# MLP up-projection: eight products with the weights' high part, then eight with the low part

## The chip, the cores and the metric

The kernel runs on one core of one Trainium2 chip. The metric is device time in microseconds (us). A core has five engines with an instruction stream each: the tensor engine (PE in the profile, with its weight loads listed apart as PEld), the vector engine (DVE), the scalar engine (ACT), GpSimd (POOL) and the sync engine (SP), which here issues the DMAs that bring the weights. Products accumulate in PSUM, which the vector and the scalar engine read.

## The reference

Two layers ("layer 0" and "layer 1" below) of a mixer and an MLP over 256 tokens of width 1024, all in float32. The mixer (three kinds of attention and their gates) is not touched. Of the MLP this is what is computed:

```python
def squared_relu_mlp(h, w_up, w_down):          # h (256, 1024), w_up (1024, 4096), w_down (4096, 1024)
    return jnp.square(jax.nn.relu(h @ w_up)) @ w_down
...
        h = rms_norm(x, mlp_norm[l])
        x = x + squared_relu_mlp(h, w_mlp_up[l], w_mlp_down[l])
```

## The kernel before

Every float32 operand is held as a rounded high part and the remainder, the low part, and a product of two such operands is made of three: high times high, high times low, low times high. `three` (lines 210, 211, 212) issues them one behind the other. A weight tile of 512 KB is fetched by a DMA on SP's queue into one of four `raw` buffers, and split by `fetch`: ACT writes the high part (L190, six `whi` buffers) and DVE the low part (L191, six `wlo` buffers).

The MLP goes over 32 tiles f of 128 of the 4096 hidden columns. `up(f)` multiplies tile f's weights with the normalised activations `xm`, k running over eight blocks of the width. `xm.both(k)` is 512 wide, 256 columns of the activations' high part and 256 of their low part, so that one product with the weights' high part (L873, 512 wide) does two of the three, and a second with the low part (L874, 256 wide) the third. Both go into one PSUM tile `u`, named `pup`, of which there are four. For each k the two stand side by side: high, low, high, low. The last tile, f = 31, is done with `three` (`project_t`), whose products are 256 wide here.

`squared_relu(f)` brings the tile out of PSUM: ACT copies one half (L880), DVE adds the other (L881) and applies relu and the norm's row `xm.row` (L882), ACT squares (L883) and rounds to the high part (L229), DVE takes the low part (L230). The result is `h2[f]`, named `sq`. `down(w, h2, t, half, f)` multiplies it with the down-projection's weights into one of four accumulators (quarters, two token blocks by two column halves): three 512 wide products each, twelve for each f. The loop runs `down` two tiles behind `up`, so that a repetition of the middle of the MLP is twelve products of `down` and sixteen of `up`.

At the head of the MLP three tiles of `up` are issued ahead of the loop; between the products of the second stand the two products of the norm's statistics (`xm.stats`, L275, four rows in the profile) and between those of the third the transposes that turn the norm into a row (`xm.stats_row`, L313). At the end the four last tiles of `down` (f = 28 to 31) are done by quarter, in the order that `ends` writes: the first quarter with f = 28, 29 and 30, the second with f = 28, the first with f = 31, the second with the rest, then the third and the fourth. In layer 0, ACT copies a quarter that is done (`copied`, L938), PE transposes it one quarter later (`turned`, L944) and DVE adds it to the residual.

The order on each engine is set by a planner, which takes the instructions that are ready by its own estimate of time; only from the end of the MLP on (`order_pe`) is PE's order the written one. In layer 1 the planner also has four groups of four transposes (`x_rows`, L902) among the repetitions. Each engine executes its instructions in order.

Of the kernel before, what the change touches and what calls it, by code (L numbers as in the profile page):

```python
# [15 lines left out]
S = 256  # L16
NT = S // P
L = 2
KD = D // P
# [106 lines left out]
def trunk(ctx: ExitStack, tc: tile.TileContext, x, wts, consts, gains, gfin, xtok, out):  # L126


    nc = tc.nc
# [34 lines left out]
    def load_w(*key):  # L164

        ahead = 0 if key[:2] == (0, "b0") else AHEAD
        while order and len(loaded) < ahead + 1:
            first = order.pop(0)
            loaded[first] = fetch(first)
        return loaded.pop(key)  # L170
# [29 lines left out]
    def misc_tile(name="misc"):  # L200
        return ps.tile([P, 512], F32, name=name, tag="misc", bufs=4)
# [142 lines left out]
    def project_t(l, key, n, xn, o):  # L344

        wh, wl = load_w(l, key, n, 0)
        for k in range(KD):
            xh, xl = xn.k(k)
            three(o, wh[:, k, :], wl[:, k, :], xh, xl, k == 0, k == KD - 1)
# [175 lines left out]
    def layer(l, xn, before):  # L525
# [300 lines left out]
        xm = []  # L826
# [31 lines left out]
        xm = xm[0]  # L858
# [4 lines left out]
        def up(f, between=None):  # L863

            u = misc_tile("pup")
            if f >= NF - WHOLE:
                project_t(l, "up", f, xm, u[:, 0:S])
                return u
            wh, wl = load_w(l, "up", f, 0)
            for k in range(KD):  # L870
                if between and k in between:
                    between[k]()
                nc.tensor.matmul(u, wh[:, k, :], xm.both(k), start=k == 0, stop=False)  # L873
                nc.tensor.matmul(u[:, 0:S], wl[:, k, :], xm.k(k)[0], start=False, stop=k == KD - 1)  # L874
            return u

        def squared_relu(f, u):
# [10 lines left out]
        def down(w, h2, t, half, f):  # L888

            sl, cs = slice(P * t, P * t + P), slice(512 * half, 512 * half + 512)  # L890
            three(
                accs[2 * t + half], h2[0][:, sl], h2[1][:, sl], w[0][:, 0, cs], w[1][:, 0, cs], f == 0, f == NF - 1
            )
# [15 lines left out]

        h2 = {}  # L910
        first = [up(f, {1: {4: lambda: xm.stats(accs[3])}, 2: {4: xm.stats_row}}.get(f)) for f in range(LAG + 1)]
        for f in range(NF):
            h2[f] = squared_relu(f, first[f] if f <= LAG else up(f))
            if LAG <= f < NF - ENDS + LAG:
                w = load_w(l, "down", f - LAG, 0)
                for q in quarters:
                    down(w, h2[f - LAG], *q, f - LAG)
            if last and f in (8, 12, 16, 20):
                x_rows(*quarters[(f - 8) // 4])
# [4 lines left out]
        def finish(q, fs):  # L924
            for i in fs:
                down(ws[i], h2[NF - ENDS + i], *quarters[q], NF - ENDS + i)


        ends = [lambda: (finish(0, range(3)), finish(1, range(1)), finish(0, range(3, 4)))]
        ends += [lambda: finish(1, range(1, 4)), lambda: finish(2, range(4)), lambda: finish(3, range(4))]  # L930

        if not last:
            xn = Normed(G_ATT + KD * (l + 1))
# [85 lines left out]
    for l in range(L):  # L1019
        xn, before = layer(l, xn, before)  # L1020
# [85 lines left out]
```

## Time and profile before

| | us |
|---|---|
| three timed runs | 861.53, 861.37, 861.49; median 861.49 |
| the profiled execution | 861.24 |
| its span, first to last instruction | 859.5 |
| layer 0's MLP, first `up` product to the first product of its end | 248.79 to 417.07 |
| layer 1's MLP, likewise | 672.13 to 841.96 |

The profile is of one execution. A row of the timeline gives an instruction's start and its duration, both in us, the engine, the line, the operation, what it writes and reads, and its shape. Products on PE are pipelined: each is listed as longer than the distance to the next, so the distance from start to start (called the pitch below) is what a product costs, and the durations overlap. A bracket at the end of a row is the time in which the engine was idle before it, and what ended that.

### The profile page before, as it was taken

How to read it: one execution, taken by the hardware profiler on the slowest of the kernel's cores; microseconds unless marked ns; L12 is line 12 of the kernel's file. 1: busy time of each engine (PE TensorE's matmuls, PEld its weight loads, DVE VectorE, ACT ScalarE, POOL GpSimd, SP SyncE). 2: the span in 40 equal slices, each digit the busy share in tenths (PEclk: the TensorE clock that was granted, in tenths of full speed). 3: DMA queues.
4: the chain of work that ended last, by engine and by line, in shares of the span. 5: the costliest groups of instructions: out<-in, count | busy, mean ns of one | idle time of the engine just before them, and what ended most of it. 6: DMA issues, size and time to landing. Idle time of an engine off the chain costs nothing.

```text
span 859.5 us, 12496 instructions
## 1 busy us (share of the span) xinstructions
PE 849.2 (99%) x4544; PEld 728.8 (85%) x4544; DVE 618.1 (72%) x1198; ACT 507.7 (59%) x885; POOL 12.1 (1%) x23
## 2 busy tenths in 40 slices
PE   8999999999999999999999999999999999999997
PEld 7888888988898888888888888889889988888885
DVE  6896787787777666666589767977877776666664
ACT  7766776535456555555577567665355565555553
POOL 0000000000000000000000000000100000000000
PEclk9999999999999999999999999999999999999999
DMA  9775344446366665555356455445565666666641
GB/s 339 235 233 172 124 147 140 148 155 194 126 196 195 202 192 192 183 188 192 109 202 213 153 159 163 139 140 168 150 194 148 174 205 191 190 182 185 196 123 50
DMA packets 42541, 150.08 MB, mean 175 GB/s; under 512 B 4848, under 2 KB 5360, under 8 KB 42480
## 3 DMA queue, kind: packets, MB, share of 16 engines
q1 hardware_dynamic: 42192, 149.13, 55.7%
q8 instruction: 36, 0.59, 0.3%
q10 hardware_dynamic: 288, 0.16, 0.1%
q14 instruction: 25, 0.20, 0.1%
HBM read 148.22 MB, written 1.05 MB: 174 GB/s over the span
## 4 chain that ended last, share of the span: by engine, by line
PE 96%; DVE 1%; ACT 1%; issue 1%; DMA 1%; SPq 0%; POOLq 0%; POOL 0%; ACTq 0%
PE acc L210 22%; PE acc L211 22%; PE acc L212 22%; PE pup L873 13%; PE pup L874 7%; PE po L428 2%; PE ps_s L666 1%; PE ps_pt L421 1%; PE ps_s L388 1%; PE po L429 1%; DMA raw<-wts 1%; ACT whi L190 0%; PE pqk L686 0%; DVE wlo L191 0%; PE ps_r L388 0%
## 5 line engine op out<-in xcount | busy, mean ns | idle before, releaser
L191 DVE TENSOR_TENSOR wlo<-raw,whi 128x1024 fp32r<-128x1024 f32 (+2 forms) x279 | 336.3, 1209 | 164.2 <-ACT whi L190 162.3
L190 ACT ACTIVATE whi<-raw 128x1024 fp32r<-128x1024 f32 (+2 forms) x279 | 292.0, 1048 | 257.7 <-PE acc L212 152.0
L873 PE MATMUL pup<-xs,whi 128*128 128x512 f32 x496 | 176.9, 398 | 0.0
L211 PE MATMUL acc<-wlo,xs 128*128 128x512 f32 (+1 forms) x384 | 151.8, 395 | 0.6 <-DVE wlo L191 0.6
L210 PE MATMUL acc<-whi,xs 128*128 128x512 f32 (+1 forms) x384 | 150.7, 397 | 0.4 <-ACT whi L190 0.3
L212 PE MATMUL acc<-whi,xs 128*128 128x512 f32 (+1 forms) x384 | 150.7, 393 | 0.0
L874 PE MATMUL pup<-xs,wlo 128*128 128x256 f32 x496 | 138.3, 280 | 0.0
L873 PEld LDWEIGHTS pup<-xs,whi 128*128 128x128 f32 x496 | 92.9, 188 | 21.3
L210 PE MATMUL acc<-whi,sq 128*128 128x512 f32 x256 | 101.5, 397 | 0.4 <-ACT sq L229 0.4
L211 PE MATMUL acc<-wlo,sq 128*128 128x512 f32 x256 | 100.0, 391 | 0.0
L212 PE MATMUL acc<-whi,sq 128*128 128x512 f32 x256 | 99.5, 393 | 0.0
L874 PEld LDWEIGHTS pup<-xs,wlo 128*128 128x128 f32 x496 | 93.6, 189 | 2.2
L210 PEld LDWEIGHTS acc<-whi,xs 128*128 128x128 f32 x384 | 72.2, 188 | 14.3 <-ACT whi L190 1.5
L211 PEld LDWEIGHTS acc<-wlo,xs 128*128 128x128 f32 x384 | 72.3, 188 | 14.1 <-DVE wlo L191 1.6
L212 PEld LDWEIGHTS acc<-whi,xs 128*128 128x128 f32 x384 | 72.3, 188 | 13.0
L212 PEld LDWEIGHTS acc<-whi,sq 128*128 128x128 f32 x256 | 47.9, 188 | 11.7 <-DVE sq L230 0.2
L210 PEld LDWEIGHTS acc<-whi,sq 128*128 128x128 f32 x256 | 48.0, 188 | 11.2 <-ACT sq L229 0.8
L211 PEld LDWEIGHTS acc<-wlo,sq 128*128 128x128 f32 x256 | 48.2, 188 | 8.8
L211 PE MATMUL acc<-mTl,whi 128*128 128x256 f32 x128 | 36.3, 284 | 1.0 <-DVE mTl L230 1.0
L210 PE MATMUL acc<-mTh,whi 128*128 128x256 f32 x128 | 36.2, 285 | 0.0
L212 PE MATMUL acc<-mTh,wlo 128*128 128x256 f32 x128 | 36.1, 283 | 0.0
L410 ACT ACTIVATE prob<-prob,smx 128x128 f32<-128x128 f32 x64 | 28.3, 445 | 7.5 <-DVE smx L407 7.2
(241 smaller groups left out, 1196.3 us busy)
## 6 DMA issues: line engine op xcount, KB each, us to landing
raw<-wts SPq DMA_DIRECT2D x268, 512.0 KB, 3.7
raw<-wts SPq DMA_DIRECT2D x7, 416.0 KB, 3.3
xrow<-xtok SPq DMA_DIRECT2D x4, 256.0 KB, 8.4
y<-y SPq DMA_DIRECT2D x4, 256.0 KB, 2.2
DEC<-consts SPq DMA_DIRECT2D x1, 768.0 KB, 7.5
x<-x SPq DMA_DIRECT2D x1, 512.0 KB, 6.3
raw<-wts SPq DMA_DIRECT2D x2, 256.0 KB, 3.7
gf<-gfin SPq DMA_DIRECT2D x1, 512.0 KB, 3.9
```

The source lines that it names most:

```text
L190: nc.scalar.activation(hi[:, :sz], raw[:, :sz], AF.Copy)
L191: nc.vector.tensor_sub(lo[:, :sz], raw[:, :sz], hi[:, :sz].bitcast(F32))
L210: nc.tensor.matmul(o, ah, bh, start=start, stop=False)
L211: nc.tensor.matmul(o, ah, bl, start=False, stop=False)
L212: nc.tensor.matmul(o, al, bh, start=False, stop=stop)
L388: nc.tensor.matmul(o, b if swap else a, a if swap else b, start=i == 0, stop=i == 1)
L410: nc.scalar.activation(p[:, a:b], p[:, a:b], AF.Exp, bias=m[:, 2 + i : 3 + i], scale=scale, accum_out=m[:, 4 + i : 5 + i])
L421: nc.tensor.transpose(pt[:, P * i : P * i + P], got["p"][:, src : src + P], ident)
L428: nc.tensor.matmul(dst, v[0], pT[:, 0:S], start=True, stop=False)
L429: nc.tensor.matmul(dst[:, P:S], v[1], pT[:, S : 3 * P], start=False, stop=True)
L873: nc.tensor.matmul(u, wh[:, k, :], xm.both(k), start=k == 0, stop=False)
L874: nc.tensor.matmul(u[:, 0:S], wl[:, k, :], xm.k(k)[0], start=False, stop=k == KD - 1)
```

## The change

For every tile but f = 0 and f = 31, `up` issues the eight products with the weights' high part first and then the eight with the low part. For f = 0 the order stays side by side, and f = 31 isn't concerned. The statistics and the row's transposes stand before the fifth high product, as before, so now with no low product ahead of them. No product is added or removed, and shapes, operands and buffers stay the same. In `ends`, the second quarter's f = 29 moves ahead of the first quarter's f = 31; the two layers share that list.

```diff
-            for k in range(KD):
-                if between and k in between:
-                    between[k]()
-                nc.tensor.matmul(u, wh[:, k, :], xm.both(k), start=k == 0, stop=False)
-                nc.tensor.matmul(u[:, 0:S], wl[:, k, :], xm.k(k)[0], start=False, stop=k == KD - 1)
+
+            jobs = [(part, k) for part in range(2) for k in range(KD)]
+            for part, k in sorted(jobs, key=lambda job: job[1]) if f == 0 else jobs:
+                if part == 0:
+                    if between and k in between:
+                        between[k]()
+                    nc.tensor.matmul(u, wh[:, k, :], xm.both(k), start=k == 0, stop=False)
+                else:
+                    nc.tensor.matmul(u[:, 0:S], wl[:, k, :], xm.k(k)[0], start=False, stop=k == KD - 1)
             return u
...
-        ends = [lambda: (finish(0, range(3)), finish(1, range(1)), finish(0, range(3, 4)))]
-        ends += [lambda: finish(1, range(1, 4)), lambda: finish(2, range(4)), lambda: finish(3, range(4))]
+        ends = [lambda: (finish(0, range(3)), finish(1, range(2)), finish(0, range(3, 4)))]
+        ends += [lambda: finish(1, range(2, 4)), lambda: finish(2, range(4)), lambda: finish(3, range(4))]
```

What the planner makes of it stands in the built programs. On PE, with H for a high and l for a low product of `up`, 0, 1 and 2 for the three 512 wide products of `down`, s for the statistics and r for the row's transposes, the head of the MLP and its first repetitions are (both layers alike, but for layer 1's `x_rows`):

```
before  HlHlHlHlHlHlHlHlHlHlHlHlHlHHlHllHlHlHlHlHHlssHllHlHlHlHlHlHlHlHlHlrr
        HlHlHlHlHlHlHlHlHlHlHlHlHlHlHlHlH01010101lHlHlHlHlHl2222012012... (40 of down in all) HlHl
        012012012012HlHlHlHlHlHlHlHl012012012012HlHlHlHlHlHlHlHl ...
after   HlHlHlHlHlHlHHHHHHHHHHHHHHHHlHHHHHHHlHllssllllllHllllllllHllllllllrr
        HHHHHHHHllllllllHHHHHHHHllllllllHHHHHHHH01010101llll2222012012... (40 of down in all) llll
        012012012012HHHHHHHHllllllll012012012012HHHHHHHHllllllll ...
```

On ACT, in a repetition, the squaring (L883) now stands ahead of the next weight tile's split (L190) where it stood behind it; at the end of layer 0 tile 30's squaring and rounding likewise stand ahead of the second 832 wide split. On DVE a few instructions change places at the head and one at the end of layer 0. The order on SP and POOL, and everything outside the two MLPs, is the same.

## The prediction

> **What bounds the kernel now.** I read the page first: the busy shares, then the chain that ended last by engine and line, then the costliest groups.
>
> ```profile
> PE 849.2 (99%) x4544; PEld 728.8 (85%) x4544; DVE 618.1 (72%) x1198; ACT 507.7 (59%) x885; POOL 12.1 (1%) x23
> ...
> PE 96%; DVE 1%; ACT 1%; issue 1%; DMA 1%; SPq 0%; POOLq 0%; POOL 0%; ACTq 0%
> ...
> L873 PE MATMUL pup<-xs,whi 128*128 128x512 f32 x496 | 176.9, 398 | 0.0
> ...
> L874 PE MATMUL pup<-xs,wlo 128*128 128x256 f32 x496 | 138.3, 280 | 0.0
> L873 PEld LDWEIGHTS pup<-xs,whi 128*128 128x128 f32 x496 | 92.9, 188 | 21.3
> ```
>
> The tensor engine (PE) is the bound: 96% of the chain, and no idle time ahead of either line of the change. So two things can move the end: the distance from one product's start to the next (the pitch), and the few places where PE waits. The listed 398 and 280 ns overlap and are not the price. I took the pitch from PE's timeline, in one repetition of layer 0's MLP, and then in two places that show what the new order will be made of.
>
> ```profile
> 282.73 0.39 PE L873 MATMUL pup<-xs,whi 128*128 128x512 f32 x1
> ...
> 333.07 0.39 PE L873 MATMUL pup<-xs,whi 128*128 128x512 f32 x1
> ...
> 335.88 0.40 PE L210 MATMUL acc<-whi,sq 128*128 128x512 f32 x1
> ...
> 338.66 0.39 PE L873 MATMUL pup<-xs,whi 128*128 128x512 f32 x1
> ...
> 411.38 0.39 PE L873 MATMUL pup<-xs,whi 128*128 128x512 f32 x1
> ```
>
> From 282.73 to 411.38 lie 23 repetitions: 128.65 / 23 = 5.593 us each, without variation (333.07 to 338.66 is 5.59). Of that the eight pairs take 335.88 - 333.07 = 2.81, and the twelve products of the down-projection 338.66 - 335.88 = 2.78.
>
> ```profile
> 272.00 0.39 PE L211 MATMUL acc<-wlo,sq 128*128 128x512 f32 x1
> ...
> 279.03 0.39 PE L212 MATMUL acc<-whi,sq 128*128 128x512 f32 x1
> ```
>
> The same down-projection products, 32 in a row with no 256 wide ones near: 31 distances in 7.03 us, a pitch of 0.2268. Twelve should take 2.72, not 2.78: behind the alternating pairs, the 512 wide products run slow for a while.
>
> ```profile
> 467.29 0.28 PE L210 MATMUL acc<-cTh,whi 128*128 128x256 f32 x1
> ...
> 468.24 0.28 PE L212 MATMUL acc<-cTh,wlo 128*128 128x256 f32 x1
> ...
> 470.04 0.28 PE L212 MATMUL acc<-cTh,wlo 128*128 128x256 f32 x1
> 470.16 0.40 PE L210 MATMUL acc<-whi,xs 128*128 128x512 f32 x1
> ...
> 472.68 0.39 PE L212 MATMUL acc<-whi,xs 128*128 128x512 f32 x1
> ```
>
> This is a mixer stage whose order is like the new one: an even train of 512 wide products, then 24 of 256, then 512 again. The first eight short ones take 468.24 - 467.29 = 0.95 us, and the pitch stays at 0.12 (470.04 to 470.16). The next eleven distances take 472.68 - 470.16 = 2.52, where 11 x 0.2268 = 2.495: a step from short to long costs about 0.025 once and fades.
>
> **The change part by part.**
>
> A repetition. Nothing is added or removed: eight 512 wide and eight 256 wide products and as many weight loads stay. New sum: eight high at 0.2268 = 1.81, eight low 0.95, twelve down 2.52 + 0.227 = 2.75; together 5.51 against 5.593, so 0.08 less. With the front's scheme, 24 such repetitions stand in each layer's steady part. In four of layer 1's, transposes break the train already:
>
> ```profile
> 717.25 0.60 PE L902 MATMUL pxr<-K,x 128*128 128x128 f32 x4
> ```
>
> There I count half: 46 x 0.08 = 3.7 us. Bounds: if the fading after each step is as long as behind pairs (2.78 instead of 2.75 for the twelve), 0.05 and 2.3 us; if the eight low products in a row cost what they cost within pairs (2.81 - 8 x 0.2268 = 1.00), 0.03 and 1.4 us; if both, nothing. Upper end: 5.50, both at the even pitch (20 x 0.2268 + 8 x 0.12), 4.4 us. I take 3.7, since 467 to 473 us has just this pattern.
>
> What hides the rest of a repetition: the copy from PSUM (L880) waits for a tile's last low product in both programs, so it comes no earlier; the squaring moves ahead of a weight split on the scalar engine (ACT), which splits into six buffers and mostly waits for PE to free one. A repetition needs two splits, a rounding, a squaring and a copy:
>
> ```profile
> L190 ACT ACTIVATE whi<-raw 128x1024 fp32r<-128x1024 f32 (+2 forms) x279 | 292.0, 1048 | 257.7 <-PE acc L212 152.0 <-PE pup L873 55.9 <-PE acc L211 21.5
> ...
> L229 ACT ACTIVATE sq<-relu 128x256 fp32r<-128x256 f32 x64 | 25.9, 415 | 1.6
> L883 ACT ACTIVATE relu<-relu 128x256 f32<-128x256 f32 x64 | 25.2, 403 | 5.8 <-DVE relu L882 5.8
> L880 ACT COPY relu<-pup 128x256 f32<-128x256 f32 x62 | 21.5, 354 | 1.0 <-PE pup L874 1.0
> ```
>
> 2 x 1.05 + 0.42 + 0.40 + 0.35 = 3.3 of 5.5 us on ACT, whose idle time ahead of the splits is put down to PE, and a tile's result is needed only two tiles later. If that cover were gone, each us lost on ACT beyond 2.2 would show on PE, 48 times. On SP's queue the same loads stand in the same order; 1 MB per repetition in 1.5% less time is no new load beside the 339 GB/s that the page's first slice shows:
>
> ```profile
> GB/s 339 235 233 172 124 147 140 148 155 194 126 196 195 202 192 192 183 188 192 109 202 213 153 159 163 139 140 168 150 194 148 174 205 191 190 182 185 196 123 50
> ```
>
> The head of the MLP.
>
> ```profile
> 248.79 0.40 PE L873 MATMUL pup<-xs,whi 128*128 128x512 f32 x1
> ...
> 256.40 0.50 PE L275 MATMUL acc<-ones,sqsum 128*128 128x1 f32 x4
> ...
> 260.44 0.38 PE L313 MATMUL acc<-K,ms 128*128 128x128 f32 x2
> ```
>
> Before the statistics stand 22 high and 21 low products: 22 x 0.2268 + 21 x 0.12 = 7.51, and they took 7.61. In the new order 30 high and 10 low stand there, 8.0 us, so the statistics come some 0.5 later; but only 2 high and 22 low follow before the row's transposes, 3.1 instead of 3.67, and those come at 260.4 as now. Tile 0 is complete after 29 high and 8 low: 7.54 + 0.1, at 256.4 as now. The vector engine (DVE) frees its PSUM buffer at
>
> ```profile
> 249.96 1.23 DVE L191 TENSOR_TENSOR wlo<-raw,whi 128x1024 fp32r<-128x1024 f32 x1 [0.21 <-ACT whi L190]
> ...
> 258.72 0.42 DVE L881 TENSOR_TENSOR relu<-pup,relu 128x256 f32<-128x256 f32 x1
> ```
>
> 259.14, and the fifth tile needs it behind the transposes, after 260.5: no wait. The weights of tiles 1 to 3, whose high products now run ahead, are split before the first step is over (the last of six at 251.2). With fewer steps between widths I take 0.1 per layer, 0.2 in all; bounds 0 and 0.3.
>
> The end of layer 0's MLP, the one long stop of PE in it.
>
> ```profile
> 414.07 0.28 PE L874 MATMUL pup<-xs,wlo 128*128 128x256 f32 x1
> ...
> 414.27 0.90 ACT L190 ACTIVATE whi<-raw 128x832 fp32r<-128x832 f32 x1 [0.88 <-PE pup L873]
> ...
> 415.07 0.35 ACT L880 COPY relu<-pup 128x256 f32<-128x256 f32 x1
> ...
> 415.20 1.03 DVE L191 TENSOR_TENSOR wlo<-raw,whi 128x832 fp32r<-128x832 f32 x1 [0.97 <-ACT whi L190]
> ...
> 417.15 0.90 ACT L190 ACTIVATE whi<-raw 128x832 fp32r<-128x832 f32 x1 [1.73 <-PE pup L211]
> ...
> 417.96 0.70 ACT L883 ACTIVATE relu<-relu 128x256 f32<-128x256 f32 x2
> ...
> 418.22 0.39 PE L212 MATMUL acc<-whi,sq 128*128 128x512 f32 x1
> 418.57 0.71 ACT L229 ACTIVATE sq<-relu 128x256 fp32r<-128x256 f32 x2
> 419.02 0.50 PE L210 MATMUL acc<-whi,sq 128*128 128x512 f32 x1 [0.41 <-ACT sq L229]
> ...
> 419.36 0.39 PE L211 MATMUL acc<-wlo,sq 128*128 128x512 f32 x1
> ```
>
> PE's seventh product of the end needs tile 30's rounding. That stood on ACT behind a split which waited until 417.15 for a buffer that tile 31 freed. The stop is (0.80 - 0.227) + (0.34 - 0.227) = 0.69 us. In the new order tile 30's high products end 0.95 earlier, the first 832 wide split with them (it waited for L873), the copy follows tile 30's end (414.2) directly, and squaring and rounding stand ahead of the second split: copy 0.35, DVE's split 1.03 beside it, two DVE steps and two ACT steps of 0.4 each, 3 us with the handovers, so ready near 417.2 against 418.45 wanted. I count the whole 0.7, bounds 0 and 0.7. Late next would be tile 31: it is wanted two triples after tile 30's now, three with the change, which is what the new `ends` gives (0.68 more); I cost that line at nothing, since its own cover, tile 31's rounding, is there in both orders. Moved past it: the first quarter's copy to its transposes,
>
> ```profile
> 421.41 0.59 ACT L938 COPY ydn<-acc 128x512 f32<-128x512 f32 x1 [2.13 <-PE acc L212]
> ...
> 423.25 0.60 PE L944 MATMUL pyd<-K,ydn 128*128 128x128 f32 x4
> ```
>
> now 1.84 from the copy's start to the transposes with 0.59 needed; with a triple less, 1.16: still hidden. Layer 1's end has no transposes and no such stop.
>
> Sum: 3.7 + 0.2 + 0.7 = 4.6 us from the profiled execution's 861.24, so 856.6; the median of the runs is 861.49, 0.25 above, and gives 856.9.
>
> The trace's pitch of 0.2268 depends on what ran before. The Trainium skill ("TensorE: Matmul & The Clock Gate", section "Back-to-back issue gap") has a warm gap of N / 2.4 + 2.5 ns by the width N alone, 215.8 ns for 512 and 109.2 for 256; the trace has 226.8 and 120, and up to 2% more after a step. By that rule the order of the products could change nothing and the sum would be the 0.7 of the stop; this is the second rival below.
>
> **The rivals.**
>
> Long fading: the 512 wide products run slow behind eight short ones as long as behind pairs. For it: 2.78 in every repetition now. Against it: 470.16 to 472.68. It gives 2.3 + 0.2 + 0.7 = 3.2 less, 858.3.
>
> The order is worth nothing on PE: the 0.09 per repetition stick to the place (the neighbours' reads and writes), not to the pairs. For it: the even train at 272 us runs while no pair is there, but also while ACT and DVE have other work. Then only the stop goes: 860.8, not measurable.
>
> Slower: the head stalls. All four PSUM buffers are open while 30 high products run ahead, and the fifth tile's first product waits for tile 0's release. Now that has 260.58 - 259.14 = 1.4 us to spare. Every us beyond costs two, in two layers; it decides once the release is later by 1.4 + (4.6 + 1.7) / 2 = 4.6 us. Against it: tile 0 ends at the same time as now and ACT's order there is unchanged up to the row. At 6 us late: 861.5 - 4.6 + 9.2 = 866.
>
> Eight weight loads in a row behind short products, each listed at 188 ns, would make 0.19 of the pitch; 467.29 to 470.16, where 24 loads stand so, excludes it.
>
> **How the numbers follow.** Forecast 0.71; long fading 0.14; nothing on PE 0.07; slower 0.04; better than forecast (upper bounds together, 856.1) 0.04. About 0.2% (1.7 us) is what a measurement of this kernel tells from no change, and the first two and the last of the cases are beyond it: faster 0.89, same 0.07, slower 0.04. The likeliest gives 856.9. The range takes the upper bounds with the runs' spread at the low end, 855.8, and the long fading with a smaller share of the stop at the high end, 858.9.
>
> **What would show it.** Right: a repetition of 5.51 us in the steady part, twelve down products in 2.75, no idle time near the end's seventh product, and the row's transposes at 260.4. Wrong: a repetition still at 5.59 (then pairs weren't the cause), a pitch over 0.12 within the low products, or idle time of PE before L876 at the head.

## The result, and the profile after

The changed kernel takes 857.61 us (median of five runs, 857.33 to 857.84) against 861.53 (861.37 to 862.01) for the kernel before on the same chip: 0.9952 of the time, 95% interval 0.9940 to 0.9964. The prediction was 856.9, with a range from 855.8 to 858.9. The profiled execution took 857.82, its span 856.0 (861.24 and 859.5 before).

From the page of the changed kernel: the busy shares, the chain, and the two lines of the change in the costliest groups.

```profile
PE 845.4 (99%) x4544; PEld 729.7 (85%) x4544; DVE 618.4 (72%) x1198; ACT 508.6 (59%) x885; POOL 13.9 (2%) x23
...
PE 96%; DMA 1%; DVE 1%; issue 1%; ACT 1%; POOLq 0%; POOL 0%; ACTq 0%
...
L876 PE MATMUL pup<-xs,whi 128*128 128x512 f32 x496 | 125.1, 391 | 0.0
...
L878 PE MATMUL pup<-xs,wlo 128*128 128x256 f32 x496 | 72.2, 282 | 0.0
```

PE is still 96% of the chain, with as many products as before. Its busy time fell by 3.8 us. The groups' 125.1 and 72.2 us (176.9 and 138.3 before) must not be read as a gain of 118 us: durations overlap, and in a train of like products less of each is put down to its group. The distance from start to start is what counts. PE's timeline of the changed kernel, one repetition, and the first and last of 23:

```profile
283.55 0.39 PE L876 MATMUL pup<-xs,whi 128*128 128x512 f32 x1
...
333.17 1.98 PE L876 MATMUL pup<-xs,whi 128*128 128x512 f32 x8
334.98 1.11 PE L878 MATMUL pup<-xs,wlo 128*128 128x256 f32 x8
335.93 0.40 PE L210 MATMUL acc<-whi,sq 128*128 128x512 f32 x1
...
338.68 1.98 PE L876 MATMUL pup<-xs,whi 128*128 128x512 f32 x8
...
410.35 0.39 PE L876 MATMUL pup<-xs,whi 128*128 128x512 f32 x1
```

(410.35 - 283.55) / 23 = 5.513 us a repetition, against 5.593. Its parts are 1.81 (eight high), 0.95 (eight low) and 2.75 (twelve of the down-projection).

The end of layer 0's MLP, ACT and PE:

```profile
412.37 0.90 ACT L190 ACTIVATE whi<-raw 128x832 fp32r<-128x832 f32 x1 [0.45 <-PE pup L876]
...
413.32 0.37 ACT L884 COPY relu<-pup 128x256 f32<-128x256 f32 x1
...
415.23 0.42 ACT L887 ACTIVATE relu<-relu 128x256 f32<-128x256 f32 x1 [1.53 <-DVE relu L886]
...
415.68 0.42 ACT L229 ACTIVATE sq<-relu 128x256 fp32r<-128x256 f32 x1
...
416.00 0.40 PE L210 MATMUL acc<-whi,sq 128*128 128x512 f32 x1
...
416.08 0.90 ACT L190 ACTIVATE whi<-raw 128x832 fp32r<-128x832 f32 x1
...
417.39 0.39 PE L210 MATMUL acc<-whi,sq 128*128 128x512 f32 x1
...
420.31 0.59 ACT L942 COPY ydn<-acc 128x512 f32<-128x512 f32 x1 [2.57 <-PE acc L212]
...
421.47 0.60 PE L948 MATMUL pyd<-K,ydn 128*128 128x128 f32 x4
```

Tile 30's squaring (415.23) and rounding (415.68) now stand ahead of the second 832 wide split (416.08). PE's seventh product (417.39) has no bracket: the stop of 0.69 us is gone. From the quarter's copy to its transposes lie 1.16 us.

Where the time went, in distances that I took from the starts of the same products in both traces (us):

| | before | after | difference |
|---|---|---|---|
| layer 0: first high product to first steady down product (head) | 31.16 | 31.11 | -0.05 |
| layer 0: the 24 steady repetitions | 134.24 | 132.32 | -1.92 |
| layer 0: the 24 down products of its end that hold the stop | 6.184 | 5.471 | -0.71 |
| layer 0's first high product to layer 1's | 423.333 | 420.640 | -2.69 |
| layer 1: its repetitions | 135.80 | 134.21 | -1.59 |
| layer 1's first high product to the last product of all | 180.514 | 178.880 | -1.63 |

The two long distances together are 4.33 us shorter, but the spans differ by only 3.43 (859.46 and 856.03). The rest lies ahead of both MLPs: layer 0's first high product starts at 248.79 before and at 249.69 after, and PE's 100th product already comes 0.92 us later, counted from its first (25.90 us against 24.98). PE's waits in the first 16 us (total, count, longest), of the kernel before and then of the changed one:

```profile
PE acc L211 <- DVE wlo L191: 0.6, 1, 0.6
PE acc L210 <- ACT whi L190: 0.3, 1, 0.3
```

```profile
PE acc L211 <- DVE wlo L191: 1.1, 2, 0.6
PE acc L210 <- ACT whi L190: 0.7, 1, 0.7
```

PE waits there for the splits of the very first weights, 0.9 us longer in the second trace. The change touches no instruction that runs by then, so this is scatter. In eleven more profiles, below, the 100th product comes 25.14 to 27.40 us after the first, with 25.45 and 25.64 in two more of the changed kernel itself; the profile of before had the earliest of all. The median of the timed runs fell by 3.92, between the two figures.

### The profile page after: what moved, and what is told of

Read it like the earlier page. It is cut to its first block, busy times and chain, and to the rows that moved or that the text cites. A ratio compares the mean times of both kernels' runs of the same rounds, so it can differ in the third digit from the quotient of the medians.

```text
span 856.0 us, 12494 instructions
## 1 busy us (share of the span) xinstructions
PE 845.4 (99%) x4544; PEld 729.7 (85%) x4544; DVE 618.4 (72%) x1198; ACT 508.6 (59%) x885; POOL 13.9 (2%) x23
## 4 chain that ended last, share of the span: by engine, by line
PE 96%; DMA 1%; DVE 1%; issue 1%; ACT 1%; POOLq 0%; POOL 0%; ACTq 0%
PE acc L211 22%; PE acc L210 22%; PE acc L212 22%; PE pup L876 13%; PE pup L878 7%; PE po L428 2%; PE ps_s L666 1%; PE ps_pt L421 1%; DMA raw<-wts 1%; PE ps_s L388 1%; PE po L429 1%; PE pqk L686 0%; DVE wlo L191 0%; PE ps_r L388 0%; ACT whi L190 0%
## 5 line engine op out<-in xcount | busy, mean ns | idle before, releaser
L190 ACT ACTIVATE whi<-raw 128x1024 fp32r<-128x1024 f32 (+2 forms) x279 | 292.0, 1049 | 171.6 <-PE acc L212 80.8
L876 PE MATMUL pup<-xs,whi 128*128 128x512 f32 x496 | 125.1, 391 | 0.0
L887 ACT ACTIVATE relu<-relu 128x256 f32<-128x256 f32 x64 | 26.2, 415 | 88.3 <-DVE relu L886 88.3
L878 PEld LDWEIGHTS pup<-xs,wlo 128*128 128x128 f32 x496 | 68.9, 190 | 4.8
L878 PE MATMUL pup<-xs,wlo 128*128 128x256 f32 x496 | 72.2, 282 | 0.0
```

Of the source, the lines that this page charges most:

```text
L190: nc.scalar.activation(hi[:, :sz], raw[:, :sz], AF.Copy)
L887: nc.scalar.activation(s, s, AF.Square)
```

## The experiments

My theory was the prediction's: alternating short and long products slow the 512 wide ones; each step from short to long costs a little that fades (0.025 us behind a short train); and the stop goes because tile 30's rounding gets ahead of a split on ACT. Rivals: the gain sticks to something else in the new order; the new `ends` made it or a part of it; the stop goes by `ends` and not by tile 30. To get rid of the scatter at the start, each run is read by the distances of the table (layer 0's first high product to layer 1's, and from there to the last product) beside its time.

**The two edits apart.** `old_ends` is the changed kernel with the old list, `only_ends` the kernel before with the new one; `after_again` is the changed kernel unaltered, on the chip of `old_ends`.

```diff
 old_ends (against the changed kernel)
-        ends = [lambda: (finish(0, range(3)), finish(1, range(2)), finish(0, range(3, 4)))]
-        ends += [lambda: finish(1, range(2, 4)), lambda: finish(2, range(4)), lambda: finish(3, range(4))]
+        ends = [lambda: (finish(0, range(3)), finish(1, range(1)), finish(0, range(3, 4)))]
+        ends += [lambda: finish(1, range(1, 4)), lambda: finish(2, range(4)), lambda: finish(3, range(4))]
 only_ends (against the kernel before): the same two lines, the other way round
```

> The changed kernel once more, for the first 15 us. In its first profile PE's order and every distance up to the first MLP are as before, but between 8 and 13 us three waits for the first weights were longer and everything behind is 0.9 us late. Theory 'scatter of the first loads': in another execution the lateness is another one (anything from 0 to 1 us), and the span moves by just that, between 855.1 and 856.1. Rival 'the changed kernel starts later': again 0.9 us late at 15 us. In both, a repetition is 5.513 us and the end of layer 0's MLP has no stop; the time lies between 856.8 and 857.8.

> The changed order of the products, with the old order of the four last tiles of the down-projection. Theory 'the second edit is worth nothing': tile 31's rounding is done before either order wants it, no stop of PE at the end of layer 0's MLP, time as the changed kernel within 0.1 us. Rival 'the second edit took the stop away': a wait of 0.3 to 0.7 us for tile 31's or tile 30's result comes back, time 0.3 to 0.7 above the changed kernel.

> The new order of the end with the old order of the products. Theory 'the second edit is worth nothing by itself': repetitions of 5.593, the stop of 0.7 us at the seventh product stays, since the third triple is the same in both orders; time of the kernel before within 0.1 us. Rival: the stop gets shorter by a triple (0.68) and the time is 860.8.

`after_again` took 857.57 us, 0.9947 (0.9935 to 0.9960); `old_ends` 857.49, 0.9948 (0.9934 to 0.9961). Layer 0's distance is 420.646 with the old list and 420.640 with the new, both without the stop. `only_ends` took 861.63, 0.9998 (0.9989 to 1.0007), with 423.333 in layer 0 as in the kernel before, and the stop is there at PE's seventh product:

```profile
417.50 0.90 ACT L190 ACTIVATE whi<-raw 128x832 fp32r<-128x832 f32 x1 [1.73 <-PE pup L211]
...
418.92 0.71 ACT L229 ACTIVATE sq<-relu 128x256 fp32r<-128x256 f32 x2
...
419.37 0.50 PE L210 MATMUL acc<-whi,sq 128*128 128x512 f32 x1 [0.41 <-ACT sq L229]
```

So the second edit is worth nothing in either order. All the gain is in the order of `up`.

**Tile 30 apart.** `not30` leaves tile 30 side by side and does the rest as changed; `only30` has the new order in tile 30 alone.

```diff
 not30
-            for part, k in sorted(jobs, key=lambda job: job[1]) if f == 0 else jobs:
+            for part, k in sorted(jobs, key=lambda job: job[1]) if f in (0, NF - 2) else jobs:
 only30
-            for part, k in sorted(jobs, key=lambda job: job[1]) if f == 0 else jobs:
+            for part, k in sorted(jobs, key=lambda job: job[1]) if f != NF - 2 else jobs:
```

> The changed kernel, but tile 30 has its products side by side as before. The planner then puts tile 30's squaring on ACT behind the second 832 wide split again. Theory 'the stop went because tile 30's squaring stands ahead of that split': the wait of PE at the seventh product of the end of layer 0's MLP is back, about 0.6 to 0.7 us. Rival 'it went because the earlier tiles release their buffers sooner': no wait. Repetitions of 5.513 us in both.

> Side by side as before for all tiles but tile 30, which has eight high and then eight low products; the end in the new order. Theory: repetitions of 5.593 us, no stop at the end of layer 0's MLP, so 0.7 us below the kernel before (860.8). Rival: the stop stays and the time is that of the kernel before.

`not30` has the repetition of 5.513, and the stop again. Its ACT and PE at the end of layer 0:

```profile
417.64 0.90 ACT L190 ACTIVATE whi<-raw 128x832 fp32r<-128x832 f32 x1 [1.73 <-PE pup L211]
...
419.06 0.71 ACT L229 ACTIVATE sq<-relu 128x256 fp32r<-128x256 f32 x2
...
419.51 0.50 PE L210 MATMUL acc<-whi,sq 128*128 128x512 f32 x1 [0.41 <-ACT sq L229]
```

Layer 0's distance is 421.413, 0.77 more than with the change: 0.71 of the stop, and 0.05 in tile 30's own sixteen products. Its single run took 860.23, which says little, since in its profile the 100th product came 27.40 us after the first, the latest of all; the waits of its first 18 us have

```profile
PE acc L210 <- ACT whi L190: 1.9, 2, 1.2
```

`only30` keeps 5.593 in the other tiles and loses the stop:

```profile
417.32 0.42 ACT L229 ACTIVATE sq<-relu 128x256 fp32r<-128x256 f32 x1
...
417.72 0.90 ACT L190 ACTIVATE whi<-raw 128x832 fp32r<-128x832 f32 x1
...
419.03 0.39 PE L210 MATMUL acc<-whi,sq 128*128 128x512 f32 x1
```

Layer 0 takes 422.579, 0.754 less than before. The time is 861.15, 0.9995 (0.9986 to 1.0004): 0.5 us below the kernel before on that chip, too little for the timed runs to tell. The stop thus hangs on tile 30's own order, and not on the earlier tiles. That order is worth 0.75 of the 4.33 us in layer 0: the stop's 0.71, and 0.05 of tile 30's own sixteen products.

**How the products must be grouped.** If a step from short to long costs a fixed amount, fours (two steps a tile) should stand between eights (one) and pairs (eight), and twos (four steps) nearer to the pairs.

```diff
 group4 (group2: // 2)
-            for part, k in sorted(jobs, key=lambda job: job[1]) if f == 0 else jobs:
+            for part, k in sorted(jobs, key=lambda job: (job[1] if f == 0 else job[1] // 4, job[0])):
```

> Four high, four low, four high, four low: two steps from short to long products per repetition instead of one (and eight before). Theory 'each step costs': the second step costs what is left of the fading after four products, 0.02 to 0.03, so a repetition of 5.53 to 5.54 us. Rival 'only strict alternation is slow': 5.51 as with eight. Rival 'the number of steps doesn't count, the fading behind the last one does': 5.51 or 5.55, with the twelve down products at 2.75 or 2.78.

> Two high, two low, four times: four steps per repetition. Theory 'each step costs': 5.55 to 5.57 us, between 5.51 (one step) and 5.593 (eight). Rival 'only strict alternation is slow': 5.51. If a step cost the same however short the runs are, (5.593 - 5.513) / 7 = 0.0115 each, so 5.55 here and 5.525 with groups of four.

PE's timeline of `group4`, a repetition, and then the same of `group2`:

```profile
333.09 1.07 PE L876 MATMUL pup<-xs,whi 128*128 128x512 f32 x4
334.00 0.64 PE L878 MATMUL pup<-xs,wlo 128*128 128x256 f32 x4
334.47 1.09 PE L876 MATMUL pup<-xs,whi 128*128 128x512 f32 x4
335.40 0.63 PE L878 MATMUL pup<-xs,wlo 128*128 128x256 f32 x4
335.87 0.40 PE L210 MATMUL acc<-whi,sq 128*128 128x512 f32 x1
...
338.64 1.07 PE L876 MATMUL pup<-xs,whi 128*128 128x512 f32 x4
```

```profile
333.29 0.61 PE L876 MATMUL pup<-xs,whi 128*128 128x512 f32 x2
333.74 0.40 PE L878 MATMUL pup<-xs,wlo 128*128 128x256 f32 x2
333.98 0.63 PE L876 MATMUL pup<-xs,whi 128*128 128x512 f32 x2
...
336.07 0.40 PE L210 MATMUL acc<-whi,sq 128*128 128x512 f32 x1
...
338.80 0.62 PE L876 MATMUL pup<-xs,whi 128*128 128x512 f32 x2
```

Over 23 repetitions, fours take 5.547 us and twos 5.507, a little less than eights; 5.53 to 5.54 and 5.55 to 5.57 had been expected. With fours, four high products behind four low ones take 335.40 - 334.47 = 0.93, against 334.00 - 333.09 = 0.91 behind other 512 wide products, and twelve down products 2.77: the step costs some 0.02 each time. With twos, two high behind two low take 0.47 against 0.45, so the step costs too; but the eight low products take 0.92 together by their starts, against 0.95, and the twelve down products only 2.73. Their single runs took 859.67 (fours) and 858.40 (twos). Both have the stop at the end of layer 0 again: the 24 down products that hold it take 6.19 us in both, 0.72 and 0.71 more than with the change, with tile 30's rounding behind the second split on ACT. With fours the squaring is ahead of that split and the rounding behind it, and PE waits at the ninth product, for the low part that DVE takes from the rounded one:

```profile
416.04 0.42 ACT L887 ACTIVATE relu<-relu 128x256 f32<-128x256 f32 x1 [1.63 <-DVE relu L886]
...
416.48 0.90 ACT L190 ACTIVATE whi<-raw 128x832 fp32r<-128x832 f32 x1
...
417.29 0.40 ACT L229 ACTIVATE sq<-relu 128x256 fp32r<-128x256 f32 x1
...
418.83 0.50 PE L212 MATMUL acc<-whi,sq 128*128 128x512 f32 x1 [0.37 <-DVE sq L230]
```

A fixed price for each step is refuted: one, two, four and eight steps a tile cost 5.513, 5.547, 5.507 and 5.593.

**Fewer steps, and twos without the stop.** `two_tiles` issues, from f = 3 on, two tiles together: sixteen high, sixteen low, then 24 down products, half a step a tile. `group2_30` has twos, but eights in tile 30.

```diff
 two_tiles
+        def up_two(f):
+            us = [misc_tile("pup") for _ in range(2)]
+            ws = [load_w(l, "up", f + i, 0) for i in range(2)]
+            for i in range(2):
+                for k in range(KD):
+                    nc.tensor.matmul(us[i], ws[i][0][:, k, :], xm.both(k), start=k == 0, stop=False)
+            for i in range(2):
+                for k in range(KD):
+                    nc.tensor.matmul(us[i][:, 0:S], ws[i][1][:, k, :], xm.k(k)[0], start=False, stop=k == KD - 1)
+            return us
...
+            if f > LAG and f % 2 and f < NF - 1:
+                two[f], two[f + 1] = up_two(f)
-            h2[f] = squared_relu(f, first[f] if f <= LAG else up(f))
+            h2[f] = squared_relu(f, first[f] if f <= LAG else two[f] if f in two else up(f))
 group2_30
-            for part, k in sorted(jobs, key=lambda job: job[1]) if f == 0 else jobs:
+            for part, k in sorted(jobs, key=lambda job: (job[1] if f == 0 else job[1] // (8 if f == NF - 2 else 2), job[0])):
```

> From tile 3 on two tiles of the up-projection together: sixteen high, sixteen low, then 24 products of down. One step for two repetitions. Theory 'each step costs 0.02 net': two repetitions take 32 x 0.2268 + ... = 11.006 instead of 11.026, 0.02 less, 12 times a layer, 0.5 us in all: 857.1. Rival 'the planner or the scalar engine makes a wait of it': two results come at once and ACT and DVE are late; PE then idles before a down product and the time is 857.6 or more.

> Two high, two low in turn for all tiles but 30, which has eight and eight. From the traces so far a repetition in twos takes 5.507 us (5.513 with eights), but tile 30 in twos brought the stop of 0.7 back, since the planner put its squaring behind the second 832 wide split. Theory 'each of the two edits acts where it was seen': repetitions of 5.507, no stop, and behind the first loads a program 0.2 to 0.3 us shorter than the changed kernel. Rival 'the stop hangs on the earlier tiles too': it stays, 0.4 above the changed kernel.

> Two tiles together once more, beside the changed kernel on the same chip: two repetitions 11.007 us, 0.4 to 0.5 below the changed kernel in the median, if the scatter of the first loads lets it show.

> The changed kernel beside the two others: repetitions of 5.513 us, no stop; only the first 15 us differ from its other profiles, by 0 to 1 us.

The sixteen and sixteen of `two_tiles` on PE:

```profile
338.21 3.79 PE L921 MATMUL pup<-xs,whi 128*128 128x512 f32 x16
341.84 2.08 PE L924 MATMUL pup<-xs,wlo 128*128 128x256 f32 x16
343.75 0.40 PE L210 MATMUL acc<-whi,sq 128*128 128x512 f32 x1
```

Two repetitions take 11.007 us, where twice the change's 5.513 is 11.026: one step fewer saves 0.02, as the fading behind a train of short products lets expect. The two distances are 420.432 and 178.688, together 0.40 below the changed kernel's. `group2_30` has 5.507, no stop, and 420.546 and 178.688, 0.29 below. Times: `two_tiles` 856.98, 0.9943 (0.9930 to 0.9955); then, on one other chip, `two_tiles_b` (the same kernel) 857.11, 0.9945 (0.9931 to 0.9958), `group2_30` 857.25, 0.9946, and `after_third` (the changed kernel) 857.67, 0.9955 (0.9942 to 0.9967). The traces put both versions ahead of the changed kernel, and the medians are in the same order. The intervals overlap: 0.4 us is less than the scatter of the first loads.

## Why the prediction was right, point by point

*A repetition: 5.51 predicted, 5.513 measured*, with all three parts (1.81, 0.95, 2.75) as read from the mixer stage at 467 us. Of the bounds, neither long fading (2.78 for twelve) nor dearer low products (1.00 for eight) came. That the order makes the difference is shown by the kernels that change nothing else: 5.593, 5.547, 5.513 and 5.507 with the same 28 products of the same widths. The rival by which the order is worth nothing on PE falls with them. The rule that stood beside it is given in its source for an isolated product (the Trainium skill, "TensorE: Matmul & The Clock Gate", "Back-to-back issue gap"); the prediction took it for a rule of a stream. In this stream, with a weight load for each product, the trace disagrees with it: 226.8 ns where it gives 215.8, and 5.593 and 5.513 us for products of equal widths.

The starts of single products show where the time lay. In the pairs before, the eight high products took 1.88 us and the eight low ones 0.93, so the bound with 1.00 for the low products had put the extra on the wrong ones: alternation slows the 512 wide products, to as much as 241 ns instead of 227 (6%, more than the 2% that the prediction names, which is a mean over twelve). Behind the eight low products (at 335.93 us) the next 512 wide ones take 234, 235, 229, 232 and 231 ns and then 227, and behind the 24 short ones in the mixer stage (at 470.16 us, the kernel before) they take the same. Beside them ACT is busy for 0.58 us of these 1.4 us in the first place and for 1.23 in the second, and the DMA share is 0.49 and 0.81. So the slowing goes with what PE ran before, and not with the neighbours' work.

*46 such repetitions, 3.7 us: 3.51 measured.* The step that was mis-sized is "There I count half", for the four repetitions behind layer 1's transposes. Layer 1's repetitions gained 1.59, which is 20 x 0.08: the four gained nothing. Here is one of them in the kernel before, and then one in the changed kernel, with the transposes right ahead of the first row in both:

```profile
717.61 0.48 PE L873 MATMUL pup<-xs,whi 128*128 128x512 f32 x1
...
720.51 0.40 PE L210 MATMUL acc<-whi,sq 128*128 128x512 f32 x1
...
723.25 0.39 PE L873 MATMUL pup<-xs,whi 128*128 128x512 f32 x1
```

```profile
715.57 2.10 PE L876 MATMUL pup<-xs,whi 128*128 128x512 f32 x8
...
718.46 0.40 PE L210 MATMUL acc<-whi,sq 128*128 128x512 f32 x1
...
721.21 1.98 PE L876 MATMUL pup<-xs,whi 128*128 128x512 f32 x8
```

The sixteen products of `up` take 2.90 before and 2.89 after, the twelve behind them 2.75 in both (2.747 before by the unrounded starts). The four such repetitions take 5.65, 5.60, 5.65 and 5.60 before, 5.63, 5.62, 5.63 and 5.62 after. Before, the twelve already ran as fast behind these pairs as behind a train; and after, the eight high products don't run evenly behind the transposes (0.31 us to the second start, then 0.22 to 0.24 each). The rows of before were in its trace and I didn't read on to them.

*The head: 0.2 predicted for both layers, 0.10 measured*, within its bounds. The order of events was as worked out, in the changed kernel's timeline:

```profile
249.69 0.40 PE L876 MATMUL pup<-xs,whi 128*128 128x512 f32 x1
...
257.78 0.50 PE L275 MATMUL acc<-ones,sqsum 128*128 128x1 f32 x4
...
261.31 0.38 PE L313 MATMUL acc<-K,ms 128*128 128x128 f32 x2
```

The statistics come 8.09 after the first high product (7.61 before; 0.5 later was forecast), the row's transposes 11.62 (11.65 before). The stall at the head, the slower rival, did not come.

*The stop: 0.7 predicted, 0.71 measured.* Its mechanism is borne out by every run: in the five kernels that put tile 30's rounding ahead of the second split (the change, `old_ends`, `only30`, `group2_30`, `two_tiles`) there is no stop, in the five that don't (before, `only_ends`, `not30`, `group4`, `group2`) there is one. The gain was nearly lost, though: "ready near 417.2" rests on ACT's order in the changed program, and with fours the planner lets the second split go ahead of tile 30's rounding. In all five kernels without the stop two things go together: tile 30's high products end earlier, and the planner puts the rounding first. In four of them the first split, which those products release, starts 0.83 earlier than before, counted from the end's first product (0.95 was forecast). In `two_tiles` it starts 0.20 later, but all of tile 30 is done twelve down products earlier. With fours the first split starts 0.34 earlier, and the stop is undiminished. So an earlier first split isn't needed, and 0.34 of it isn't enough. Whether the planner's order alone would do was not tried.

*The `ends` line: nothing predicted, nothing measured* in either direction (0.006 us in layer 0). The first quarter's copy is 1.16 us ahead of its transposes, as worked out, and remains hidden.

*The sum: 4.6 predicted, 4.33 measured* in the distances of the two MLPs: 0.2 too much in the repetitions, 0.1 in the head. *What is left:* 857.61 is 0.7 above the 856.9, and the sum explains 0.3 of it. The rest is scatter from run to run and chip to chip, which these runs don't take apart. The prediction's median of the kernel before, 861.49, was of three runs; the medians of more runs are 861.53, 861.95, 861.68 and 861.75. Where both kernels were timed on one chip, their medians differ by 3.92, 4.38 and 4.08, where the distances of the traces give 4.33.

## What to carry to other kernels

Read the cost of an order from a place of the trace that already has that order, by the distance between starts and not by the listed durations; here one stage of another part of the kernel gave the new repetition to within 0.003 us. Where the gain is multiplied by a count, look at each kind of repetition in the count: four that stood behind transposes had nothing to give. Before a profiled execution is taken as the base of a sum, look at its start: here the scatter of the first loads (0.92 us between the two main profiles) was larger than all errors of the sum.

## What was not expected of the hardware

The cost of mixing widths isn't a price for each step. A tile of `up` with twelve down products takes 5.593 us with eight steps from short to long, 5.547 with two, 5.513 with one, and 5.507 with four. Behind pairs of one high and one low the twelve down products take 2.78, behind fours 2.77, behind eights 2.75 and behind twos 2.73; behind transposes and pairs they take 2.75. By the starts of single products, the first ten of the twelve don't run evenly behind pairs (225 to 241 ns), the first nine behind fours (225 to 236), five behind eights (229 to 235), and two behind twos (233 and 231). The short products differ too: the first behind a 512 wide one takes 113 ns to the next start, those in a train 120, so eight of them take 0.95 in eights and 0.92 in twos. The length of the fading thus depends on what ran before in a way that these runs only list. No run here shows its cause.

The time from PE's first product to its 100th was between 25.0 and 27.4 us over thirteen profiles of kernels that are alike up to there. It lies in PE's waits for the first splits of weights; what makes the first weights late wasn't tried.
